# A two-layer hybrid encoder: where the down halves stand among mixed products, new block sizes, and a norm whose shift is taken from three tiles

## Chip, cores and metric

One NeuronCore of one Trainium2 chip. The metric is the device time of one execution in microseconds; lower is better. The kernel before takes 1253.96 us (median of three runs, 1253.59 to 1255.86).

## What is computed

A trunk of two layers on 544 token columns (512 of a prompt, 32 of a later chunk). A layer mixes (gated positions, latent attention and a linear recurrence), projects and normalises, and then runs a convolutional feed-forward part, which the change touches, with a second norm:

```python
up = x @ lp['ffn_w_up']
upc, ffn_conv_new = causal_dwconv(up, ffn_conv_prev, lp['ffn_conv_w'], lp['ffn_conv_b'])
g_ff, val = upc[..., :D_FF], upc[..., D_FF:]
f = (jax.nn.gelu(g_ff) * val) @ lp['ffn_w_down']
x = layer_norm(ALPHA * x + f, lp['ln2_g'], lp['ln2_b'])
```

`D_MODEL` is 1024 (8 tiles of 128 rows), `D_FF` is 2816 (22 tiles for the gate and 22 for the value), the convolution has width 3. All is float32.

## The kernel before, in words

**Precision and units.** Activations stand transposed: 128 features on the partitions, 544 tokens in two column halves of 272 (`HV`). Each float32 operand is split into a high and a low part (`split`, L78: ScalarE copies the high part, L64, VectorE subtracts for the low one, L67), and a product is three matmuls (`mm3`, lines L89 to L91). So a plain tile of the up projection is 8 x 3 = 24 matmuls per half.

**Feed-forward part** (`ffn`, L1086). The 22 gate-and-value pairs are worked in four blocks (`BLK`, L26: 6, 4, 5 and 7 pairs). Block 0 is plain: 12 up tiles, the first five of them on weights that were loaded during the first norm; the others by `unit` (L1189), which also runs `settle`: it finishes the residual tiles of the first norm, and after every second one makes a set of *mixed columns* from two of them (`mixed_x`, L1070: four sums of 272 columns and two splits of 544, tiles ta, tb, th, tl). Pairs of the other blocks are *mixed* (`seven`, L1147): with weights combined by `forms` (L1047: two 512 KB loads, three splits of 128 x 1024, one of 128 x 512 and four sums of 128 x 512 in place, tiles wupr, wfwh, wfwl) a pair takes seven half products of 12 matmuls each, in the order A12, A11, S2, S1, S3, S4, A22. S1, S2, S3 and A22 need the mixed columns. `seven` is a generator and stops twice: after A11 (the second product) and after S3 (the fifth). `post` (L1127) then does the convolution with two scalar_tensor_tensor of VectorE (L70) per tile, the gelu and the product of gate and value, whose split gives the tiles fh and fl.

**Down projection.** A block's down projection (`proj`, L966: eight units of one weight column tile each, two halves per unit, 3 matmuls per pair of the block and half; the weights are split when the unit begins, tiles wd0h to wd7l) runs as `late` during the next block: the loop at L1200 puts some halves at each of the two stops. Of the 16 halves, pair j of nk takes n, by

```python
n = 16 * (j + 1) // nk - 16 * j // nk
for c in ((n + 1) // 2, n // 2):
```

**Second norm** (`proj_ln`, L973, with `LN`, L842). The last block's down projection goes straight into the norm. Tiles 0 and 1 are made together, then 2, then 3, both halves each; `gather` (L868) sums them. After the first half of tile 4 `shift` (L880) makes the mean of the first four tiles by a matmul with ones (lnc) and subtracts it from all eight tiles on VectorE, with squares on ScalarE added up in lnq. Layer 0 does both halves of tile 4, then the first halves of tiles 5 to 7, loads and splits the weights of layer 1's first units (win0 to win2) and does the second halves; in layer 1 tiles 4 to 7 are done so. `stats` (L915) and `apply` (L943) then scale each half; layer 1 stores it. The first norm uses the same class with four tiles.

**Order and buffers.** The kernel is written against a framework that puts the instructions of each engine into an order at compile time, by its own estimate of when operands are ready; program order is the priority, and `tc.high_priority` lifts a few. Buffers are drawn from pools (`BUFS`, L52): five each for split weights (wh, wl), four for raw ones (wr), pages pg, pt, kb and pp. `FPT` (L27) names the pool of each pair's fh and fl. Five PSUM banks serve the products.

Of the kernel before, what the change touches and what calls it, by code (L numbers as in the profile page):

```python
# [9 lines left out]
AF = mybir.ActivationFunctionType  # L10
ALU = mybir.AluOpType
# [8 lines left out]
HW = 272  # L20
# [2 lines left out]
PG = 550  # L23
D_FF = 2816
NI = 22
BLK = ((0, 6), (6, 4), (10, 5), (15, 7))  # L26
FPT = ("", "ggpp", "", "ggppp")  # L27
KO = (0, 2, 4, 6, 1, 3, 5, 7)
ALPHA = (2.0 * DEPTH) ** 0.25
SCALE = 96 ** -0.5  # L30
# [3 lines left out]
C_LN1G, C_LN1B, C_LN2G, C_LN2B = 0, 8, 16, 24  # L34
# [12 lines left out]
def trunk_kernel(ctx: ExitStack, tc: tile.TileContext, i, o, k):  # L47
# [6 lines left out]
    def page(name, dt=F32, tag="pg"):  # L54
        return pool.tile([128, W if tag == "pp" else PG], dt, tag=tag, name=name, bufs=BUFS[tag])

    def bank(name, tag="ps"):
        return psum.tile([128, 512], F32, tag=tag, name=name, bufs={"ps": 5, "ss": 3}[tag])
# [4 lines left out]
    def act(out, in_, func=AF.Copy, **kw):  # L63
        return nc.scalar.activation(out=out, in_=in_, func=func, **kw)  # L64

    def tt(out, a, b, op, e=None):
        return (e or nc.vector).tensor_tensor(out=out, in0=a, in1=b, op=op)  # L67

    def stt(out, a, s, b, op0, op1):
        return nc.vector.scalar_tensor_tensor(out=out, in0=a, scalar=s, in1=b, op0=op0, op1=op1)  # L70
# [67 lines left out]
    xd = [i["x"]] + [dram.tile([8, 128, W], F32, tag=f"xd{l}", name=f"xd{l}") for l in range(1, DEPTH)]  # L138
# [75 lines left out]
    def col_weights(src, kk, name, kper=8):  # L214
        res = []
        for c in range(0, kk, kper):
            n = min(kper, kk - c)
            wh, wl = weights(src[:, 128 * c:128 * (c + n)].rearrange("p (k c) -> p k c", k=n), n, 128, name)
            for j in range(n):
                res.append((wh, wl, j))  # L220
        return res
# [618 lines left out]


    class LN:  # L842
        def __init__(self, xT, first_op, va, cg, cb, spill, final, ns, tag):
            self.x, self.op, self.va, self.cg, self.cb = xT, first_op, va, cg, cb
            self.spill = spill
            self.final = final
            self.n1 = 8 - ns
            self.tag = tag

        def warm(self):  # L850
            t = const([128, 1], F32, "warm")
            act(t, self.c[:, 0:1], AF.Abs_reciprocal_sqrt, scale=0.0, bias=ones[:, 0:1])
# [15 lines left out]
        def gather(self, m, c):  # L868
            if m == 0:
                return  # L870
            if m == 1:
                self.s = page("lns", tag=self.tag)[:, 0:W]
                tt(self.s, self.x[0][:, 0:W], self.x[1][:, 0:W], ALU.add)
                return
            s = self.s[:, c]
            tt(s, s, self.x[m][:, c], ALU.add)
            if m >= 4:
                self.square(m, c)

        def shift(self):  # L880
            s = self.s
            c = self.c = page("lnc", tag=self.tag)[:, 0:W]
            q = self.q = page("lnq", tag=self.tag)[:, 0:W]
            for h in HV:
                b = bank("lnm", "ss")
                nc.tensor.matmul(b[:, 0:HW], ones, s[:, h], start=True, stop=True)
                act(c[:, h], b[:, 0:HW], AF.Copy, scale=1.0 / 512)
            for m in (4, 0, 1, 2, 3, 5, 6, 7):
                x = self.x[m][:, 0:W]
                tt(x, x, c, ALU.subtract)  # L890
                if m == 0:
                    act(q, x, AF.Square)
                elif m in (1, 2, 3):
                    self.square(m, slice(0, W))
            stt(s, c, -4.0, s, ALU.mult, ALU.add)

        def square(self, m, c):
            t = page("lnt", tag="kb")[:, c]
# [74 lines left out]
    def proj_ln(wsrc, kts, ln, name, kper, pre, mid, ko=None):  # L973
        n1 = ln.n1
        ns = 8 - n1

        def get(m):
            w = col_weights(wsrc(m), len(kts), f"{name}{m}", kper)
            return [w[j] for j in ko] if ko else w

        for ms in ((0, 1), (2,), (3,)):
            ws = [get(m) for m in ms]
            for hv in range(2):
                for m, ps in zip(ms, mms(ws, kts, hv)):
                    ln.evac(m, hv, ps)
            if ms[0] == 0 and mid is not None:
                mid()
        def one(m, w, hv):
            ps = mms([w], kts, hv)[0]
            if m == 4 and hv == 0:  # L990
                ln.shift()
            ln.evac(m, hv, ps)

        for m in range(4, n1):
            w = get(m)
            for hv in range(2):
                one(m, w, hv)
        ws = [get(m) for m in range(n1, 8)]
        nxt = pre() if pre is not None else None
        for j in range(ns):  # L1000
            one(n1 + j, ws[j], 0)
            if j == 0:
                ln.warm()
        for j in range(ns):
            ps = mms([ws[j]], kts, 1, (lambda: ln.stats(0)) if j == 0 else ln.head if ln.final and j == ns - 1 else None, 5)[0]
            if j == 0 and not ln.final:
                ln.apply(0, range(4))
            ln.evac(n1 + j, 1, ps)
        if ln.final:
            ln.stats(1)  # L1010
            ln.apply(0)
        else:
            ln.apply(0, range(4, 8))

        def hook():
            if not ln.final:
                ln.stats(1)
            ln.apply(1)
        rest = [] if ln.final else [lambda m=m: ln.settle(m) for m in range(8)]
        return nxt, hook, rest  # L1020

    def wo_stage(l, va, pre):
        xT = []
        for m in range(8):
            x = page(f"xT{m}")
            nc.sync.dma_start(out=x[:, 0:W], in_=xd[l][m])
            if m >= 4:
                act(x[:, 0:W], x[:, 0:W], scale=ALPHA)
            xT.append(x)
        ln = LN(xT, "alpha", va, C_LN1G, C_LN1B, None, False, 3, "pp")  # L1030
        ko = [6, 7, 2, 3, 0, 4, 1, 5]

        kts = [KX[m] for m in ko]
        return xT, *proj_ln(lambda m: i["wo"][l, m], kts, ln, "wo", 8, pre, None, ko)

    def up_w(l, i_, s):
        return col_weights(i["wup"][l, NI * s + i_], 8, "wup", 8)
# [48 lines left out]
    def ffn(l, va, vf, xT, first, hook, rest, pre):  # L1086
# [7 lines left out]
        def settle():  # L1094
            if rest:
                rest.pop(0)()
                if len(rest) % 2 == 0:
                    TX.append(mixed_x(xT, len(TX)))

        late = iter(())  # L1100
        for bl, (i0, nk) in enumerate(BLK):
            fts = {}
# [24 lines left out]
            def post(tl):  # L1127
# [10 lines left out]
                else:  # L1138
                    g = ac.pop((i_, 0))
                    tt(a[:, 0:W], a[:, 0:W], g[:, 0:W], ALU.mult)  # L1140
                    tag = "p" + (FPT[bl] + "tttttt")[i_ - i0]
                    fh, fl = page("fh", F32R, tag), page("fl", F32R, tag)
# [46 lines left out]
            def unit(tl):  # L1189
                n = len(tiles) - tiles.index(tl)  # L1190
                for _ in range(-(-len(rest) // n)):
                    settle()
                w = up_w(l, *tl)
                for hv in range(2):
                    ev(tl, hv, mms([w], KU, hv)[0])

            if bl == 0:
                for tl in tiles[done:]:
                    unit(tl)
            for j in range(nk if bl else 0):  # L1200
                mix = seven(i0 + j)
                n = 16 * (j + 1) // nk - 16 * j // nk
                for c in ((n + 1) // 2, n // 2):
                    next(mix)
                    for _ in range(c):
                        next(late)
                next(mix, None)
# [3 lines left out]

            if bl < len(BLK) - 1:
                def ev2(m, hv, ps, bl=bl):
                    x = xT[m][:, HV[hv]]
                    if bl == 0:
                        stt(x, x, ALPHA, ps, ALU.mult, ALU.add)
                    else:
                        tt(x, x, ps, ALU.add)
                late = proj(wsrc, [fts[j] for j in sorted(fts)], ev2, "wd")
            else:  # L1220
                fin = l == DEPTH - 1

                def mid():
                    nc.sync.dma_start(out=o[7][l], in_=fo)

                ln = LN(xT, "add", va, C_LN2G, C_LN2B, o[0] if fin else xd[l + 1], fin, 4 if fin else 3, "pg")
                nxt = proj_ln(wsrc, [fts[j] for j in sorted(fts)], ln, "wd", 8, pre, mid)
        return nxt

# [10 lines left out]
    for l in range(DEPTH):  # L1240
        mixer(l, nxt, hook, rest)
        va, vf, kvg, sp4 = vecs[l]
        xT, nxt, hook, rest = wo_stage(l, va, lambda: pre_up(l))
# [120 lines left out]
```

## Time and profile before

| | |
|---|---|
| three runs | 1253.59, 1253.96, 1255.86 us |
| the profiled execution | 1253.95 us |
| its span, first to last instruction | 1252.1 us |
| TensorE busy | 1223.2 us (98%), 9305 matmuls |
| VectorE busy | 1013.6 us (81%) |
| ScalarE busy | 741.4 us (59%) |
| mean granted TensorE clock | 0.995 |

All instructions have times from the start of the span. PE is TensorE, DVE VectorE, ACT ScalarE, SP the queue that issues the DMAs. Matmuls are pipelined, so a single one's duration says little; how many fit into a stretch says what one costs. In layer 0 the plain block runs from 239.7 to 307.3 us, block 1 to 386, block 2 to 465.2, block 3 to 572.2, the second norm's stage from there to 632.5. Layer 1 repeats it 617 us later, and its second norm ends the program.

### The profile page before, as it was taken

The numbers are of one execution on the slowest core, as the hardware profiler recorded it, in microseconds if no ns is written. First come the engines' busy times: TensorE is split into PE (matmuls) and PEld (weight loads), VectorE is DVE, ScalarE is ACT, GpSimd is POOL, SyncE is SP. The second block draws the span as 40 slices with busy tenths as digits, with TensorE's granted clock in tenths as the row PEclk, the third lists the DMA queues.
The fourth block names the chain that finished last, engine by engine and source line by source line (L and its number), as shares of the span: only waits on it lengthen the run. The fifth ranks groups of instructions, "written<-read, shape, count | busy, mean of one in ns | idle before, by whom it ended". The sixth has DMA issues, their size and how long they took to land.

```text
span 1252.1 us, 24029 instructions
## 1 busy us (share of the span) xinstructions
PE 1223.2 (98%) x9305; PEld 1178.7 (94%) x9305; DVE 1013.6 (81%) x1932; ACT 741.4 (59%) x1616; POOL 45.7 (4%) x222
## 2 busy tenths in 40 slices
PE   9999999999999999999899999999999999999994
PEld 9999879999999999999899997899999999999994
DVE  6766977997788889886886767689968788898858
ACT  6485874496455655553465767646955455565633
POOL 2400000000000000000000100000000000000000
PEclk9999999999999999999999999999999999999998
DMA  8243434022232332325144423340213223323312
GB/s 284 75 141 98 125 104 161 18 86 72 73 110 83 95 98 89 100 77 170 46 147 136 118 85 113 118 136 18 94 60 105 65 93 93 106 83 106 114 36 73
DMA packets 51043, 125.16 MB, mean 100 GB/s; under 512 B 7784, under 2 KB 13928, under 8 KB 50928
## 3 DMA queue, kind: packets, MB, share of 16 engines
q1 hardware_dynamic: 50928, 123.62, 31.8%
q8 instruction: 73, 1.20, 0.4%
q14 instruction: 42, 0.34, 0.1%
HBM read 113.17 MB, written 5.97 MB: 95 GB/s over the span
## 4 chain that ended last, share of the span: by engine, by line
PE 82%; DVE 8%; ACT 7%; issue 1%; DMA 0%; SPq 0%; ACTq 0%; DVEq 0%
PE mm L89 22%; PE mm L90 21%; PE mm L91 21%; ACT wfwh L64 2%; PE ov L255 2%; DVE xT L70 2%; ACT ac L64 1%; PE ol L255 1%; PE pT L132 1%; ACT xp L64 1%; DVE ac L70 1%; PE s L89 1%; DVE wupr L67 1%; DVE xT L67 1%; PE kv L396 1%
## 5 line engine op out<-in xcount | busy, mean ns | idle before, releaser
L64 ACT ACTIVATE wfwh<-wupr 128x1024 fp32r<-128x1024 f32 (+1 forms) x128 | 121.7, 951 | 122.6 <-PE mm L90 66.1
L67 DVE TENSOR_TENSOR wfwl<-wupr,wfwh 128x1024 fp32r<-128x1024 f32 (+1 forms) x128 | 139.4, 1089 | 14.3 <-ACT wfwh L64 13.0
L89 PE MATMUL mm<-th,wfwh 128*128 128x272 f32 x512 | 148.4, 291 | 0.0
L90 PE MATMUL mm<-tl,wfwh 128*128 128x272 f32 x512 | 147.4, 288 | 0.0
L91 PE MATMUL mm<-th,wfwl 128*128 128x272 f32 x512 | 146.4, 288 | 0.0
L70 DVE SCALAR_TENSOR_TENSOR ac<-xp,vf,ac 128x544 f32<-128x544 f32 x176 | 136.1, 781 | 8.0 <-ACT xp L64 7.2
L90 PE MATMUL mm<-xl,wfwh 128*128 128x272 f32 x384 | 111.1, 289 | 0.0
L91 PE MATMUL mm<-xh,wfwl 128*128 128x272 f32 x384 | 111.1, 289 | 0.0
L89 PE MATMUL mm<-xh,wuph 128*128 128x272 f32 x384 | 109.5, 291 | 1.5 <-DVE xT L67 1.5
L89 PE MATMUL mm<-xh,wfwh 128*128 128x272 f32 x384 | 110.9, 289 | 0.0
L90 PE MATMUL mm<-xl,wuph 128*128 128x272 f32 x384 | 110.3, 289 | 0.0
L91 PE MATMUL mm<-xh,wupl 128*128 128x272 f32 x384 | 110.3, 288 | 0.0
L89 PEld LDWEIGHTS mm<-th,wfwh 128*128 128x128 f32 x512 | 96.3, 188 | 1.2 <-ACT u L64 0.8
L90 PEld LDWEIGHTS mm<-tl,wfwh 128*128 128x128 f32 x512 | 96.6, 189 | 0.0
L91 PEld LDWEIGHTS mm<-th,wfwl 128*128 128x128 f32 x512 | 96.3, 189 | 0.0
L67 DVE TENSOR_TENSOR wupr<-wupr 128x512 f32<-128x512 f32 x128 | 88.2, 689 | 2.4
L89 PEld LDWEIGHTS mm<-xh,wuph 128*128 128x128 f32 x384 | 71.7, 188 | 2.3 <-DVE xT L67 1.9
L91 PEld LDWEIGHTS mm<-xh,wfwl 128*128 128x128 f32 x384 | 72.4, 189 | 0.0
L90 PEld LDWEIGHTS mm<-xl,wuph 128*128 128x128 f32 x384 | 72.4, 189 | 0.0
L89 PEld LDWEIGHTS mm<-xh,wfwh 128*128 128x128 f32 x384 | 72.4, 188 | 0.0
L90 PEld LDWEIGHTS mm<-xl,wfwh 128*128 128x128 f32 x384 | 72.3, 188 | 0.0
L91 PEld LDWEIGHTS mm<-xh,wupl 128*128 128x128 f32 x384 | 72.3, 188 | 0.0
(517 smaller groups left out, 4006.9 us busy)
## 6 DMA issues: line engine op xcount, KB each, us to landing
wupr<-in_wup_dram SPq DMA_DIRECT2D x88, 512.0 KB
xT<-in_x_dram SPq DMA_DIRECT2D x14, 272.0 KB
xd<-xT SPq DMA_DIRECT2D x8, 272.0 KB
xT<-xd SPq DMA_DIRECT2D x8, 272.0 KB
out_dram<-xT SPq DMA_DIRECT2D x16, 136.0 KB
ckT<-in_ckT_dram SPq DMA_DIRECT2D x8, 256.0 KB
cr<-in_ck_dram SPq DMA_DIRECT2D x8, 256.0 KB
win0r<-in_win_dram SPq DMA_DIRECT2D x8, 192.0 KB
```

The lines of the kernel that those rows point to most:

```text
L64: return nc.scalar.activation(out=out, in_=in_, func=func, **kw)
L67: return (e or nc.vector).tensor_tensor(out=out, in0=a, in1=b, op=op)
L70: return nc.vector.scalar_tensor_tensor(out=out, in0=a, scalar=s, in1=b, op0=op0, op1=op1)
L89: nc.tensor.matmul(ps, lh, rh, start=start, stop=False, **kw)
L90: nc.tensor.matmul(ps, lh, rl, start=False, stop=False, **kw)
L91: lastmm[0] = nc.tensor.matmul(ps, ll, rh, start=False, stop=stop, **kw)
L132: nc.tensor.transpose(out, in_, ident[0:p, 0:p])
L255: nc.tensor.matmul(ps, a, b, start=start, stop=stop)
L396: nc.tensor.matmul(b[0:n, 0:288], XL[j][:, cs], wh[:, ci, :], start=False, stop=False)
```

## The change

Blocks are 5, 5, 5 and 7 pairs: one pair per layer passes from the plain block to a mixed one, and `FPT` names a pool for block 1's fifth pair. Of the halves of the previous block's down projection, one stands behind A11 in every pair; the others stand behind S3. The number of halves done by the end of a pair is odd, except after a block's last pair, so that the half behind A11 is the second one of its unit in all pairs but the first of a block. The counts are 3, 4, 2, 4, 3 for five pairs and 3, 2, 2, 2, 2, 2, 3 for seven. The second norm's mean is taken of three tiles, after the first half of tile 3; tile 3 is then gathered and squared like tiles 4 to 7. The first norm stays at four.

```diff
-BLK = ((0, 6), (6, 4), (10, 5), (15, 7))
-FPT = ("", "ggpp", "", "ggppp")
+BLK = ((0, 5), (5, 5), (10, 5), (15, 7))
+FPT = ("", "ggppt", "", "ggppp")
...
             tt(s, s, self.x[m][:, c], ALU.add)
-            if m >= 4:
+            if m >= self.n0:
                 self.square(m, c)
...
         def shift(self):
-            s = self.s
+            s, n0 = self.s, self.n0
...
-                act(c[:, h], b[:, 0:HW], AF.Copy, scale=1.0 / 512)
-            for m in (4, 0, 1, 2, 3, 5, 6, 7):
+                act(c[:, h], b[:, 0:HW], AF.Copy, scale=1.0 / (128 * n0))
+            for m in (n0, *range(n0), *range(n0 + 1, 8)):
...
-                elif m in (1, 2, 3):
+                elif m < n0:
                     self.square(m, slice(0, W))
-            stt(s, c, -4.0, s, ALU.mult, ALU.add)
+            stt(s, c, -float(n0), s, ALU.mult, ALU.add)
...
-        for ms in ((0, 1), (2,), (3,)):
+        n0 = ln.n0
+        for ms in ((0, 1), (2,), (3,))[0:n0 - 1]:
...
-            if m == 4 and hv == 0:
+            if m == n0 and hv == 0:
                 ln.shift()
...
-        for m in range(4, n1):
+        for m in range(n0, n1):
...
+            halves = 0
             for j in range(nk if bl else 0):
                 mix = seven(i0 + j)
-                n = 16 * (j + 1) // nk - 16 * j // nk
-                for c in ((n + 1) // 2, n // 2):
+                end = 16 if j == nk - 1 else 2 * round(8 * (j + 1) / nk - 0.5) + 1
+                for c in (1, end - halves - 1):
                     next(mix)
+                    halves += c
                     for _ in range(c):
                         next(late)
                 next(mix, None)
```

## Rows read from the trace of the kernel before

**Rows 1.** The page's chain of work that ended last, by engine.
```profile
PE 82%; DVE 8%; ACT 7%; issue 1%; DMA 0%; SPq 0%; ACTq 0%; DVEq 0%
```

**Rows 2.** Stretches: us, then busy us (instructions) per engine, clock, DMA share, GB/s.
```profile
core 0: us, PE busy (x) PEld busy (x) DVE busy (x) ACT busy (x) POOL busy (x), PEclk, DMA share, GB/s
239.70:307.30 67.60, 67.60 (x539) 67.54 (x538) 60.37 (x103) 53.82 (x129) 0.90 (x9) 1.00 0.21 67
307.30:386.00 78.70, 78.59 (x626) 78.35 (x625) 60.41 (x90) 39.40 (x77) 0.69 (x7) 1.00 0.26 78
386.00:465.20 79.20, 78.02 (x614) 77.18 (x613) 70.39 (x109) 46.78 (x98) 0.99 (x10) 1.00 0.32 98
465.20:572.20 107.00, 105.98 (x831) 104.51 (x830) 94.28 (x141) 64.06 (x135) 1.94 (x17) 1.00 0.34 102
...
596.40:632.50 36.10, 32.18 (x232) 31.19 (x232) 32.96 (x73) 16.64 (x34) 0.00 (x0) 0.95 0.18 49
...
1213.50:1252.10 38.60, 22.79 (x167) 21.62 (x165) 30.39 (x74) 16.27 (x36) 0.00 (x0) 0.87 0.17 59
```

**Rows 3.** PE's waits: for whom, us in total, times, longest us.
```profile
PE mm L89 <- ACT xh L64: 3.9, 1, 3.9
PE ln L908 <- DVE lns L67: 1.9, 1, 1.9
...
PE mm L89 <- ACT wd3h L64: 1.8, 4, 0.6
```

**Rows 4.** DVE's groups in block 3 of layer 0: busy us, mean ns of one, idle before.
```profile
L67 DVE TENSOR_TENSOR wfwl<-wupr,wfwh 128x1024 fp32r<-128x1024 f32 x19 | 23.2, 1219 | 0.7 <-ACT wfwh L64 0.6
...
L67 DVE TENSOR_TENSOR wupr<-wupr 128x512 f32<-128x512 f32 x24 | 16.5, 688 | 0.4
...
L67 DVE TENSOR_TENSOR xp<-xp,mm 128x272 f32<-128x272 f32 x14 | 6.1, 434 | 6.2 <-PE mm L91 6.2
...
L67 DVE TENSOR_TENSOR wfwl<-wupr,wfwh 128x512 fp32r<-128x512 f32 x6 | 4.2, 693 | 0.2
```

**Rows 5.** DVE's groups in the plain block of layer 0.
```profile
L70 DVE SCALAR_TENSOR_TENSOR ac<-xp,vf,ac 128x544 f32<-128x544 f32 x22 | 16.7, 781 | 0.5 <-ACT xp L64 0.5
L67 DVE TENSOR_TENSOR wupl<-wupr,wuph 128x1024 fp32r<-128x1024 f32 x7 | 8.5, 1220 | 0.0
...
L67 DVE TENSOR_TENSOR tl<-ta,th 128x544 fp32r<-128x544 f32 x4 | 2.9, 720 | 0.0
```

**Rows 6.** Instructions in order of time, block 3, around unit 1 of the down projection.
```profile
482.58 0.73 ACT L64 ACTIVATE wd1h<-wd1r 128x640 fp32r<-128x640 f32 x1
...
483.36 0.39 PE L89 MATMUL mm<-fh,wd1h 128*128 128x272 f32 x1 [0.32 <-ACT wd1h L64]
...
483.71 0.29 PE L89 MATMUL mm<-th,wfwh 128*128 128x272 f32 x1
```

**Rows 7.** Three stretches from A12 to the next pair's A12, block 3, columns as above.
```profile
479.85:494.73 14.88, 14.56 (x117) 14.33 (x115) 13.43 (x21) 8.90 (x20) 0.20 (x2) 1.00 0.30 94
...
526.58:541.14 14.56, 14.56 (x116) 14.38 (x115) 12.57 (x19) 8.56 (x19) 0.20 (x2) 1.00 0.29 96
541.14:555.50 14.36, 14.36 (x116) 14.36 (x115) 12.42 (x20) 8.88 (x21) 0.20 (x2) 1.00 0.32 92
```

**Rows 8.** DVE in order of time, around the plain block's end at 307.3.
```profile
302.45 1.23 DVE L67 TENSOR_TENSOR wfwl<-wupr,wfwh 128x1024 fp32r<-128x1024 f32 x1 [0.82 <-ACT wfwh L64]
...
313.29 0.72 DVE L67 TENSOR_TENSOR fl<-ac,fh 128x544 fp32r<-128x544 f32 x1
```

**Rows 9.** DVE in order of time, second norm of layer 0.
```profile
599.34 3.27 DVE L67 TENSOR_TENSOR xT<-xT,lnc 128x544 f32<-128x544 f32 x5 [3.08 <-ACT lnc L64]
...
614.15 0.43 DVE L67 TENSOR_TENSOR lnq<-lnq,lnt 128x272 f32<-128x272 f32 x1
```

**Rows 10.** The stretch behind PE's wait of 3.9 us, columns as in rows 2.
```profile
620.80:624.40 3.60, 3.60 (x16) 3.36 (x17) 3.60 (x11) 2.48 (x5) 0.00 (x0) 0.55 0.00 0
```

**Rows 11.** DVE in order of time, last norm.
```profile
1216.75 3.27 DVE L67 TENSOR_TENSOR xT<-xT,lnc 128x544 f32<-128x544 f32 x5 [4.21 <-ACT lnc L64]
...
1242.52 4.62 DVE L70 SCALAR_TENSOR_TENSOR xT<-xT,va,lnc 128x272 f32<-128x272 f32 x11
```

More of the change, by code (lines that the diff above doesn't have):

```diff
@@ L842, in trunk_kernel, with __init__ @@
     class LN:
-        def __init__(self, xT, first_op, va, cg, cb, spill, final, ns, tag):
+        def __init__(self, xT, first_op, va, cg, cb, spill, final, ns, tag, n0):
             self.x, self.op, self.va, self.cg, self.cb = xT, first_op, va, cg, cb
@@ L848, in __init__ @@
             self.tag = tag
+            self.n0 = n0
         def warm(self):
@@ L1029, in wo_stage @@
             xT.append(x)
-        ln = LN(xT, "alpha", va, C_LN1G, C_LN1B, None, False, 3, "pp")
+        ln = LN(xT, "alpha", va, C_LN1G, C_LN1B, None, False, 3, "pp", 4)
         ko = [6, 7, 2, 3, 0, 4, 1, 5]
@@ L1224, in mid @@
                     nc.sync.dma_start(out=o[7][l], in_=fo)
-                ln = LN(xT, "add", va, C_LN2G, C_LN2B, o[0] if fin else xd[l + 1], fin, 4 if fin else 3, "pg")
+                ln = LN(xT, "add", va, C_LN2G, C_LN2B, o[0] if fin else xd[l + 1], fin, 4 if fin else 3, "pg", 3)
                 nxt = proj_ln(wsrc, [fts[j] for j in sorted(fts)], ln, "wd", 8, pre, mid)
```

## The prediction

> **What bounds it now.** I read the chain of waits first: 82% of what ended last is TensorE, 8% VectorE, 7% ScalarE [rows 1]. So a change pays if it removes matmuls, or waits of TensorE. The table of stretches says where those are [rows 2]. In layer 0's plain block 539 matmuls take 67.60 us, 0.1254 us each; this is the price of a matmul that never waits. At it block 1 wants 626 x 0.1254 = 78.5 of its 78.7 us (0.2 lost), block 2 wants 77.0 of 79.2 (2.2 lost), block 3 wants 104.2 of 107.0 (2.8 lost): 5.2 us a layer. The two second norms lose most: 232 matmuls in 36.1 us, and 167 in 38.6, with VectorE busy for 32.96 and 30.39 of them. The list of TensorE's waits gives the causes [rows 3]: 3.9 us for the first normed tile in front of layer 1's input projection, 1.9 us for the last norm's sum, and many short ones for down weights not yet split.
>
> **One pair more is mixed.** A plain pair is 4 half tiles of 24 matmuls, 96; a mixed one 7 products of 12, 84. The down products stay at 22 x 8 x 2 x 3 a layer. 2 layers x 12 x 0.1254 = **3.0 us**, all on TensorE's path. VectorE pays by the means of [rows 4, 5]: the mixed pair has three wide splits, one of half width, four sums of 0.69 and three additions of 0.43, 3.66 + 0.69 + 2.75 + 1.30 = 8.4, against 2.44 for the plain pair's two splits: 6.0 more a layer. ScalarE, busy for 64 of 107 us in block 3, hides its part. DMAs: the two 512 KB loads of a pair and the 32 down loads of a layer stay, with widths 5, 5, 5, 7 for 6, 4, 5, 7; POOL's memsets stay at one per tile; on SP's queue the down loads only move among the same neighbours, and TensorE waits for no DMA in its list.
>
> **New down units go behind the fifth product.** Now the counts of halves in block 2 are (2, 1) four times and (2, 2); in block 3 (1, 1), with (2, 1) for the fourth and seventh pair; a new unit often comes first behind A11. The order on TensorE shows the price [rows 6]: the unit's high half is split on ScalarE at 482.58, TensorE waits 0.32 for it, does two of its matmuls and goes over to S2, since the low half is not there. Three pairs of block 3 have 84 + 30 = 114 matmuls, 14.30 us at the price above [rows 7]: with the new unit behind A11 it took 14.88 (0.58 lost), and with the second half behind A11 and the new unit behind S3, which the new rule makes of every pair but each block's first, 14.56 after a pair that split two units and 14.36 otherwise (0.26 and 0.06 lost). New counts are 3, 4, 2, 4, 3 halves in blocks 1 and 2 and 3, 2, 2, 2, 2, 2, 3 in block 3, always one behind A11. Of 17 pairs a layer, 7 follow a pair with two new units (three in blocks 1 and 2 each, one in block 3) and 3 begin a block; I price these ten at 0.26, the other seven at 0.06: 3.0 for 5.2, 2.2 a layer, **4.4 us**. Ends: all at 0.06 gives 4.2 a layer, 8.4; all at 0.58 in block 1, with blocks 2 and 3 as now, costs 2.7 a layer, -5.4. I take the near end because the pairs of rows 7 are the same program in the same block. Behind S3 a late unit would hold S4 and A22, and behind those the next pair's A12; ScalarE's buffer for it comes free after A11, some 6 us earlier.
>
> A block's first half down product still needs the last gated tile. In block 1 its low part ends 314.0 - 307.3 = 6.7 us after the last plain matmul [rows 8], and 24 + 12 matmuls bring TensorE there after 4.5. If nothing stood between, 2.2 us a layer; as in rows 6 the written order can put S2 and S1 there, so 0.26 to 2.2, and I take 0.26 (it is in the sum above).
>
> **The plain block has 10 tiles instead of 12.** VectorE does 60.37 us there in 67.60. Two tiles fewer take away 2 x 1.22 + 4 x 0.78 + 2 x 0.72 = 7.0 [rows 4, 5, 8], leaving 53.4 in 55.6 us: 96%. The four sets of mixed columns (four sums of 0.44 and two splits of 0.72 each, 3.2) fall on five tiles instead of seven. I cost this at nothing. The cover: the last split for the first mixed pair ends at 303.68 [rows 8]; less 7.0 that is 296.7, while S2 needs it 4.9 us (24 + 15 matmuls) after a plain block that ends at 307.3 - 12.0 = 295.3, at 300.2. 3.5 us of cover; each us beyond costs one per layer.
>
> **The second norm's shift comes a tile earlier**, 42 matmuls or 5.27 us. In layer 0 VectorE is idle for 3.08 us before the subtractions at 599.34 and then never until the sums of the first half are ready at 614.58 [rows 9]. With the shift it takes in tile 3's two additions and its sum (0.44 + 0.44 + 0.72) and the split of the first input unit (1.22), 2.8: the sums come 5.27 - 2.8 = 2.4 us sooner, and the wait of 3.9 becomes 1.5. After that wait the granted clock was 0.55, 1.2 GHz for most of 3.6 us, and 16 matmuls were done where 16 x 0.1254 = 2.0 would do [rows 10]: 1.6 lost, of which I count half back, since VectorE feeds these matmuls at about their own rate. Together **3.2 us**; ends 0 and 3.9 + 1.6 = 5.5.
>
> The Trainium skill (TensorE: Matmul & The Clock Gate, Part 1) says that an idle array falls to 1.2 GHz and comes back only with sustained work. Rows 10 agree: 0.55 right after the longest wait. By that rule the whole 1.6 comes back if the shorter wait keeps the clock, and the time would be 0.8 lower, an estimate.
>
> In the last norm the stretch starts at 1216.75 after 4.21 us idle, and the last 11 scalings run from 1242.52 to 1247.14 [rows 11]. The earlier start less tile 3's own work (1.4) is 3.9. From TensorE's side: its wait of 1.9 goes, and three scalings left over from the first half (0.42 each) are done before: 3.1. I take **3.0**; ends 0 (no bank or buffer lets the earlier start through) and 3.9. What is late next is the chain behind the last matmul, which stays.
>
> **Sum.** 3.0 + 4.4 + 3.2 + 3.0 = 13.6. The profiled execution took 1253.95 (span 1252.1 and 1.85 around it), 0.01 under the median: 1253.95 - 13.6 = 1240.4 us.
>
> **Rivals.**
> - *Slower: VectorE holds the first mixed pair.* Place: S2 after the shortened plain block. For it: 96% load, and the same backlog from the first norm in front. Price: were the first pair's weights (3 x 1.22 + 0.69 + 4 x 0.69 = 7.1) and the last mixed columns (4 x 0.44 + 2 x 0.72 = 3.2) done only after the last tile's 6.7 us, S2 would wait 6.7 + 10.3 - 4.9 = 12.1 a layer: 1240.4 + 24.2 = 1264.6. It decides from 8 us a layer (13.6 + 2.5 over two). Against it: 3.5 us of cover. 0.07.
> - *The waits only move.* New units wait behind the fifth product too, and block 1, which has none now, gets 0.58 a pair: 1253.95 - 3.0 + 5.4 - 6.2 = 1250.2. The written order may also override the placing, as in rows 6, so that the change would not do what it says. For: the pair with 14.56. Against: 14.36. 0.14.
> - *The norms gain nothing*, because five PSUM banks fill behind the longer subtractions and TensorE stops instead: 1253.95 - 7.4 = 1246.6. Against: as many half tiles stand between shift and first addition as now. 0.13.
> - My forecast 0.66.
>
> Low end: 3.0 + 8.4 + 5.5 + 3.9 = 20.8, 1233.2; the high end takes in the third rival and most of the second. Range 1234 to 1249. Within 0.2% (2.5 us, about what can be told from no change): 1251.5 to 1256.5. The second rival lies just outside it on the fast side, so part of its chance goes there: faster 0.87, same 0.06, slower 0.07.
>
> **What would show it.** Right: 24 matmuls fewer; no wait for down weights in TensorE's list but at block starts; (1, 1) pairs of 14.4 us; the subtractions about 5 us nearer the block's end; the 3.9 us wait under 2, with a clock near 1.0 after it; no 1.9 us wait at the end. Wrong: a wait of TensorE for the first mixed columns or weights of block 1; waits for down weights behind the fifth product; a wait on VectorE's additions in the norm; pairs of 15 us in block 1.

## The result and the profile after

The changed kernel takes 1240.74 us (median of four runs, 1240.62 to 1241.52) against 1254.1 in the same session: ratio 0.9894, interval 0.9878 to 0.991. The forecast was 1240.4. Its profiled execution took 1240.62, with a span of 1238.5.

From the first matmul of each stage to that of the next, us, both layers:

| stage | before | after | of it matmuls |
|---|---|---|---|
| plain block | 74.26, 74.26 | 62.23, 62.28 | -12.04 each |
| blocks 1 to 3 | 264.88, 265.17 | 273.42, 273.59 | +10.53 each |
| layer 0's second norm, to the first gating unit of layer 1 | 98.21 | 94.17 | 0 |
| last norm, to the end | 62.53 | 60.47 | 0 |

So 3.0 us are matmuls, 4.1 waits of the blocks, 4.0 and 2.1 the two norms: 13.2. (0.5 more in the spans' difference lies ahead of layer 0's plain block, which begins anywhere from 232.2 to 233.1 us in the runs below.)

The page's chain of work that ended last, by engine:

```profile
PE 89%; DVE 6%; ACT 4%; issue 1%; ACTq 0%; DVEq 0%
```

TensorE's share rose from 82% [rows 1]: what is left is more nearly matmuls alone. The stretches that answer to [rows 2], layer 0's plain block, blocks 1, 2, 3 and the norm from the shift on:

```profile
239.20:294.70 55.50, 55.50 (x443) 55.46 (x442) 53.21 (x94) 45.61 (x111) 0.59 (x6) 1.00 0.16 50
294.70:378.70 84.00, 83.69 (x663) 83.10 (x662) 69.12 (x106) 45.79 (x94) 0.99 (x10) 1.00 0.29 89
378.70:462.70 84.00, 83.19 (x663) 82.96 (x662) 73.17 (x111) 49.47 (x100) 0.99 (x10) 1.00 0.30 95
462.70:568.10 105.40, 105.26 (x830) 104.26 (x829) 92.97 (x140) 64.37 (x135) 1.88 (x18) 1.00 0.34 106
...
587.10:628.40 41.30, 39.96 (x307) 38.99 (x306) 38.15 (x84) 19.77 (x40) 0.00 (x0) 1.00 0.22 65
```

The plain block is still without a wait of TensorE, with VectorE busy for 53.21 of 55.50 us (forecast 53.4 of 55.6). At 0.1254 us a matmul the blocks lose 84.00 - 83.1 = 0.9, 0.9 and 105.40 - 104.1 = 1.3: 3.1 us for 5.2, where 3.0 was forecast. TensorE's waits:

```profile
...
PE mm L89 <- DVE xp L67: 1.6, 2, 0.8
PE mm L89 <- DVE xT L67: 1.5, 2, 0.8
PE mm L89 <- ACT xh L64: 1.3, 1, 1.3
PE mm L89 <- ACT fh L64: 0.8, 3, 0.3
```

No wait for split down weights is left [rows 3], nor the 1.9 us for the last sum; the 3.9 us for the first normed tile are 1.3. New are two waits where blocks 1 and 2 begin. In block 2, S2 waits for VectorE's addition into xp, 0.8 in each layer. In block 1, the first down half waits for the last gated tile (fh), 0.3 in each layer. TensorE in order of time: first that down half in block 1, then from A11 to S2 and unit 0 in block 2's first pair:

```profile
300.72 0.39 PE L89 MATMUL mm<-fh,wd0h 128*128 128x272 f32 x1 [0.31 <-ACT fh L64]
...
381.58 0.29 PE L91 MATMUL mm<-xh,wfwl 128*128 128x272 f32 x1
382.68 0.39 PE L89 MATMUL mm<-th,wfwh 128*128 128x272 f32 x1 [0.81 <-DVE xp L67]
382.91 0.29 PE L90 MATMUL mm<-tl,wfwh 128*128 128x272 f32 x1
383.04 0.29 PE L89 MATMUL mm<-fh,wd0h 128*128 128x272 f32 x1
```

Three pairs of block 3, a stretch of 114 matmuls from one pair's S2 to the next pair's, and the stretches around the wait of 1.3 us in layer 0's norm, which answer to [rows 7] and [rows 10]; columns as there:

```profile
479.23:493.55 14.32, 14.32 (x116) 14.32 (x115) 13.43 (x21) 9.26 (x20) 0.20 (x2) 1.00 0.30 98
493.55:507.87 14.32, 14.32 (x116) 14.32 (x115) 13.41 (x21) 9.27 (x20) 0.20 (x2) 1.00 0.29 98
507.87:522.43 14.56, 14.56 (x116) 14.38 (x115) 12.58 (x19) 8.56 (x19) 0.20 (x2) 1.00 0.31 96
...
541.69:556.54 14.85, 14.80 (x117) 14.41 (x115) 12.90 (x21) 8.41 (x19) 0.10 (x1) 1.00 0.31 89
...
611.90:614.00 2.10, 0.81 (x7) 0.59 (x5) 2.10 (x7) 0.57 (x2) 0.00 (x0) 1.00 0.00 0
614.00:617.60 3.60, 3.55 (x26) 3.33 (x27) 3.60 (x10) 2.47 (x5) 0.00 (x0) 1.00 0.00 0
```

The first two pairs take 14.32 us, as good as 114 matmuls (14.30), where [rows 7] had 14.88. Not all of block 3 is like that: the next pair takes 14.56, and the later stretch 14.85, so 0.5 of the block's 1.3 us is lost there. At block 2's start S2 follows A11 with a gap, since unit 0 of the down projection is not split yet (its low part comes at 383.94) and S2 itself waits for VectorE to read A11's bank. Behind the shorter wait of the norm the clock stays at 1.00, and 26 matmuls are done in 3.6 us instead of 16.

### The profile page after: what moved, and what is told of

Same layout as the page of the kernel before. It is cut to its first block, busy times and chain, and to the rows that moved or that the text cites. A ratio compares the mean times of both kernels' runs of the same rounds, so it can differ in the third digit from the quotient of the medians.

```text
span 1238.5 us, 24052 instructions
## 1 busy us (share of the span) xinstructions
PE 1216.6 (98%) x9281; PEld 1173.7 (95%) x9281; DVE 1020.7 (82%) x1950; ACT 745.5 (60%) x1616; POOL 44.8 (4%) x222
## 4 chain that ended last, share of the span: by engine, by line
PE 89%; DVE 6%; ACT 4%; issue 1%; ACTq 0%; DVEq 0%
PE mm L89 24%; PE mm L90 23%; PE mm L91 23%; PE ov L255 2%; DVE xT L70 1%; PE ol L255 1%; PE pT L132 1%; PE s L89 1%; DVE ac L70 1%; PE kv L396 1%; PE s L90 1%; PE kv L395 1%; PE kv L397 1%; PE s L91 1%; ACT wfwh L64 1%
## 5 line engine op out<-in xcount | busy, mean ns | idle before, releaser
L89 PE MATMUL mm<-th,wfwh 128*128 128x272 f32 x544 | 157.8, 290 | 1.6 <-DVE xp L67 1.6
L67 DVE TENSOR_TENSOR wfwl<-wupr,wfwh 128x1024 fp32r<-128x1024 f32 (+1 forms) x136 | 148.1, 1089 | 10.7 <-ACT wfwh L64 7.4
L90 PE MATMUL mm<-tl,wfwh 128*128 128x272 f32 x544 | 156.8, 289 | 0.0
L91 PE MATMUL mm<-th,wfwl 128*128 128x272 f32 x544 | 156.8, 288 | 0.0
L89 PE MATMUL mm<-xh,wuph 128*128 128x272 f32 x320 | 91.0, 291 | 1.5 <-DVE xT L67 1.5
L90 PE MATMUL mm<-xl,wuph 128*128 128x272 f32 x320 | 91.8, 288 | 0.0
L91 PE MATMUL mm<-xh,wupl 128*128 128x272 f32 x320 | 91.7, 288 | 0.0
L64 ACT ACTIVATE xp<-mm 128x272 f32<-128x272 f32 x142 | 55.0, 387 | 24.2 <-PE mm L91 24.0
L67 DVE TENSOR_TENSOR xT<-xT,mm 128x272 f32<-128x272 f32 x112 | 47.2, 434 | 17.7 <-PE mm L91 17.7
L89 PEld LDWEIGHTS mm<-xh,wuph 128*128 128x128 f32 x320 | 59.6, 188 | 2.3 <-DVE xT L67 1.9
```

The lines of the kernel that those rows point to most:

```text
L89: nc.tensor.matmul(ps, lh, rh, start=start, stop=False, **kw)
L90: nc.tensor.matmul(ps, lh, rl, start=False, stop=False, **kw)
L91: lastmm[0] = nc.tensor.matmul(ps, ll, rh, start=False, stop=stop, **kw)
```

## The experiments

All ratios are to the kernel before, timed on the same chip in the same session. The kernel before has medians of 1254.1 to 1255.4 in the sessions, so differences between runs of different sessions are given by the ratios, or by the stages of the profiles.

**One part alone: the norm.** Blocks and placing of before. Against the kernel before, written with the parameter `n0` of the change:

```diff
-                ln = LN(..., fin, 4 if fin else 3, "pg", 4)
+                ln = LN(..., fin, 4 if fin else 3, "pg", 3)
```

> The kernel before, with the second norm's shift taken from three tiles and nothing else. If the norm's gain is its own (theory): 6.2 us less than before, about 1247.9, with TensorE's 3.9 us wait for the first normed tile down to 1.3 to 1.5 and the 1.9 us wait for the last norm's sum gone. Rival, the norm gains only because the block ahead of it hands over sooner: within 1 us of before.

Measured: 1247.99, ratio 0.9945 (0.9933 to 0.9958), 6.9 us less. In its profile the norm's stages take 94.15 and 60.37, as in the changed kernel, and the other stages are those of before within 0.4. The norm's gain is its own.

**One part alone: the placing.** Blocks 6, 4, 5, 7, norm from four tiles, the new rule for the halves.

```diff
-                n = 16 * (j + 1) // nk - 16 * j // nk
-                for c in ((n + 1) // 2, n // 2):
+                end = 16 if j == nk - 1 else 2 * round(8 * (j + 1) / nk - 0.5) + 1
+                for c in (1, end - halves - 1):
```

> The kernel before, blocks 6, 4, 5, 7, with the new placing of the down halves alone. Theory (a new unit behind A11 costs about 0.5 us in the short pairs of blocks 2 and 3): 4 us less, about 1250; block 2 loses under 1 us instead of 2.2, block 3 about 1.2 instead of 2.8. Rival (the waits only move behind the fifth product): within 1 us of before.

Measured: 1248.4, ratio 0.9945 (0.9932 to 0.9957), 6.9 less, 3 more than expected. Blocks 2 and 3 of layer 0:

```profile
386.30:463.60 77.30, 77.30 (x614) 77.06 (x613) 69.69 (x109) 46.19 (x98) 0.99 (x10) 1.00 0.32 98
463.60:569.00 105.40, 105.35 (x831) 104.42 (x830) 93.76 (x141) 64.72 (x136) 1.94 (x18) 1.00 0.34 106
```

Block 2 loses 0.3 (77.30 - 77.0), block 3 1.2. The three blocks take 3.3 us less per layer, 6.6 in all. No wait for split down weights is left in TensorE's list, so the waits do not move behind the fifth product.

**One part alone: the blocks.** 5, 5, 5, 7 and the pools of the changed kernel, with the old placing and the old norm.

```diff
-BLK = ((0, 6), (6, 4), (10, 5), (15, 7))
-FPT = ("", "ggpp", "", "ggppp")
+BLK = ((0, 5), (5, 5), (10, 5), (15, 7))
+FPT = ("", "ggppt", "", "ggppp")
```

> Blocks 5, 5, 5, 7 with the old placing and the old norm. By matmuls alone 3.0 us less, 1251. If short pairs with a new unit behind A11 wait (theory), block 1's pairs, now shorter by 4.5 us, lose up to 0.58 each: 2 us a layer back, so 1253 to 1255. Rival, block 1 has room enough: 1251.

Measured: 1255.05, ratio 1.0005 (0.9996 to 1.0014): nothing. Stretches for blocks 1 and 2:

```profile
294.50:378.50 84.00, 82.82 (x652) 81.81 (x651) 68.93 (x105) 45.93 (x95) 1.00 (x10) 1.00 0.29 89
378.50:465.00 86.50, 85.66 (x673) 84.50 (x673) 73.85 (x112) 49.30 (x100) 0.99 (x10) 1.00 0.31 94
```

The plain block gives back its 12.04 us, and the blocks take 12.3 more a layer where the matmuls make 10.5: 1.8 us of waits a layer eat what the products save. They lie in block 1, which loses 84.00 - 81.8 = 2.2 where it lost 0.2; block 2 loses 2.1 as before. This is what the theory said.

**Two parts: the changed kernel without its norm part.**

```diff
-                ln = LN(..., fin, 4 if fin else 3, "pg", 3)
+                ln = LN(..., fin, 4 if fin else 3, "pg", 4)
```

> The changed kernel without its norm part (shift from four tiles). If the parts add up: 1240.7 + 6.2, about 1247. If the norm's gain depends on the blocks: under 1244 or over 1249.

Measured: 1246.89, ratio 0.9939 (0.9926 to 0.9953), 7.7 less than before. The norm adds up with it: by the ratios 5.6 us lie between this and the changed kernel. But beside the placing alone (6.9) the extra pair and the new blocks bring only about 0.8 of their 3.0 us. The intervals of the two overlap; the plain and mixed stages of the profiles give 0.9.

**Is it the split weights, or one half instead of two?** Odd numbers of halves become even, so that the one half behind A11 always begins a unit.

```diff
-                end = 16 if j == nk - 1 else 2 * round(8 * (j + 1) / nk - 0.5) + 1
+                end = 16 if j == nk - 1 else 2 * round(8 * (j + 1) / nk)
```

> The changed kernel with even numbers of halves by the end of each pair: still one half behind A11, but always the first half of a new unit, whose weights are split just then. Theory (what matters is that the half behind A11 has split weights): the waits of the old placing come back, 0.5 us for each of 14 pairs a layer, 8 to 14 us more, 1249 to 1255. Rival (one half instead of two behind A11 is what matters): within 2 us of 1240.7.

Measured: 1253.24, ratio 0.9985 (0.9976 to 0.9994), 11.4 us above the changed kernel by the ratios (blocks 1 to 3 take 12.2 more in the profiles). TensorE's waits:

```profile
PE mm L89 <- ACT wd6h L64: 5.2, 6, 1.2
PE mm L89 <- ACT wd7h L64: 2.4, 2, 1.2
PE mm L89 <- ACT wd3h L64: 2.1, 6, 0.5
```

It is the split: with the same single half behind A11, the waits for it are back, larger than in [rows 3].

**The new wait: S1 ahead of S2.** S2 adds to A11's bank and S1 opens a bank of its own; the down half moves behind S2.

```diff
-                yield
-                product(b1, f["S2"], t[2])
-                ...
                 b5 = bank("mm")
                 product(b5, f["S1"], t[0], start=True)
+                product(b1, f["S2"], t[2])
+                ...
+                yield
                 product(b1, f["S3"], t[1])
```

> The changed kernel with the products of a pair in the order A12, A11, S1, S2, then one down half, then S3 and the other halves. In the changed kernel 0.6 to 1.0 us is lost at the first S2 of blocks 1 and 2, which adds to the bank of A11 and waits for VectorE to read it; S1 has a bank of its own and would stand in between. Theory (that wait, not the weights, is what the block starts lose): 1 us less per block start in blocks 1 and 2 and a little in block 3, about 4 us in all, 1236.5 to 1238.5. Rival (VectorE is behind there anyway, the wait moves to the next product): within 1 us of 1240.7.

Measured: 1238.0, ratio 0.9861 (0.9846 to 0.9876), 4.1 us better than the changed kernel by the ratios (2.7 by the times, 3.4 by the stages of blocks 1 to 3). The waits for xp are gone from TensorE's list:

```profile
...
PE mm L89 <- DVE xT L67: 1.5, 2, 0.8
PE mm L89 <- ACT xh L64: 1.3, 1, 1.3
PE ln L909 <- DVE lns L67: 0.6, 1, 0.6
...
PE mm L89 <- ACT fh L64: 0.2, 1, 0.2
```

Blocks 1 to 3 take 271.71 us instead of 273.42. The Trainium skill (Perfetto Trace Analysis, Optimizing Tensor Performance) asks for independent products to change PSUM banks, so that reading one overlaps the next; this run agrees, with 1.7 us a layer. Not all of that need be the bank: the edit moves the down half behind S1 and S2 as well, and in block 1 the wait was for fh in front of that half. That wait is gone too (fh has 0.2 for 0.8). No run parts the two; in block 2 the line of the changed kernel names xp, the bank's reader.

**What the extra pair is worth then.** The kernel with S1 ahead of S2, with the blocks of before:

```diff
-BLK = ((0, 5), (5, 5), (10, 5), (15, 7))
-FPT = ("", "ggppt", "", "ggppp")
+BLK = ((0, 6), (6, 4), (10, 5), (15, 7))
+FPT = ("", "ggpp", "", "ggppp")
```

> S1 ahead of S2, the new placing and the norm from three tiles, with the blocks of before, 6, 4, 5, 7. If the extra mixed pair is worth its matmuls once block 1's start no longer waits (theory): 3.0 us more than with 5, 5, 5, 7, about 1241. Rival (the extra pair's worth stays below 1 us, as without S1 first): 1238 to 1239.

Measured: 1240.1, ratio 0.9884 (0.9869 to 0.9898). The pair brings 0.23%, 2.9 us by the ratios (their intervals touch; the profiles' plain and mixed stages differ by 3.0). Without S1 ahead, blocks 1 to 3 of layer 0 take 11.73 us more with the extra pair than without it (273.35 with the norm from four tiles, 261.62 with the placing alone); with S1 ahead 10.56 (271.71 for 261.15), and the matmuls make 10.53. So the waits that S1 ahead of S2 removes, at the starts of blocks 1 and 2, had taken the pair's worth.

**One pair more.** Blocks 4, 6, 5, 7 on the changed kernel.

```diff
-BLK = ((0, 5), (5, 5), (10, 5), (15, 7))
-FPT = ("", "ggppt", "", "ggppp")
+BLK = ((0, 4), (4, 6), (10, 5), (15, 7))
+FPT = ("", "ggpptt", "", "ggppp")
```

> The changed kernel with blocks 4, 6, 5, 7: one pair more passes from the plain block. By matmuls 3.0 us less, 1237.7. Theory of the slower rival of the prediction: VectorE has 46.4 us of work for 43.6 us of plain block, so TensorE waits at the first mixed pair: 1240 to 1246, with a wait of 2 us or more in front of the first S2 of block 1.

Measured: 1249.96, ratio 0.9954 (0.9938 to 0.9971), 7.5 above the changed kernel by the ratios, beyond the range I gave.

```profile
PE mm L91 <- DVE wupl L67: 4.5, 2, 2.3
PE mm L89 <- ACT wfwh L64: 3.8, 2, 1.9
PE mm L89 <- ACT wd0h L64: 1.9, 4, 0.7
```

The first wait is not where I put it: it is inside the plain block, for the low part of a plain tile's own weights (2.3 us per layer). The plain block takes 54.26 us for 50.2 us of matmuls: the wait, and a clock that falls after it. The wait for combined weights (wfwh, 1.9 per layer) stands in block 1's last pair, not at its first. ScalarE and VectorE around the wait in the plain block, the wait in block 1, and the stretches ahead of the first wait and behind it:

```profile
268.29 1.05 ACT L64 ACTIVATE wuph<-wupr 128x1024 fp32r<-128x1024 f32 x1
...
270.80 0.71 DVE L67 TENSOR_TENSOR tl<-tb,th 128x544 fp32r<-128x544 f32 x1
...
272.77 1.22 DVE L67 TENSOR_TENSOR wupl<-wupr,wuph 128x1024 fp32r<-128x1024 f32 x1
...
367.35 0.39 PE L89 MATMUL mm<-th,wfwh 128*128 128x272 f32 x1 [1.92 <-ACT wfwh L64]
```

```profile
257.90:274.00 16.10, 13.88 (x111) 13.66 (x109) 15.84 (x28) 16.07 (x46) 0.40 (x4) 1.00 0.10 35
274.00:278.00 4.00, 3.96 (x20) 3.96 (x21) 4.00 (x8) 3.18 (x7) 0.00 (x0) 0.59 0.27 71
```

The high part is there at 269.34; VectorE then does five other instructions, one of them a split of mixed columns, before it comes to the low part. VectorE is busy for 15.84 of the 16.10 us up to there, and ScalarE, which has to make the high part first, for 16.07: both are full, and which of them would have to be relieved was not tried. In the 4 us behind the first wait 20 matmuls are done, 2.5 us worth at the usual price: 1.5 us of the clock on top of the 2.3. So the load that the slower rival of the prediction feared is real one pair further on, but not its place: the first S2 of block 1 has no such wait.

**Shift from two tiles.**

```diff
-                ln = LN(..., fin, 4 if fin else 3, "pg", 3)
+                ln = LN(..., fin, 4 if fin else 3, "pg", 2)
```

> The changed kernel with the second norm's shift taken from two tiles. Theory (layer 0's norm is bound by VectorE's start, layer 1's last norm since the change by TensorE and the chain behind its last matmul): the 1.3 us wait for the first normed tile goes, 1 to 2 us less in layer 0, under 0.4 in layer 1: 1238.5 to 1240. Rival (PSUM banks fill behind the subtractions): slower by 1 us or more.

Measured: 1239.73, ratio 0.9875 (0.9861 to 0.989). Against the changed kernel's 0.9894 the times do not tell it apart; the stages do: layer 0's norm 92.79 for 94.17, with no wait for the first normed tile in the list, the last norm 60.39 for 60.47. Both as expected: the first was still waiting for VectorE, the second no longer.

**Together.** S1 ahead of S2, as above, and the shift from two tiles; against the kernel with S1 ahead:

```diff
-                ln = LN(..., fin, 4 if fin else 3, "pg", 3)
+                ln = LN(..., fin, 4 if fin else 3, "pg", 2)
```

> S1 ahead of S2 and the shift from two tiles together, on the changed kernel. If the two gains lie in different stages and add up: 1238.0 - 1.0, about 1237. Rival (the earlier hand-over of block 3 already feeds the norm): 1238.

Measured: 1236.52, ratio 0.9853 (0.9836 to 0.9869). Better than the kernel before and the changed one; against S1 first alone (0.9861) the times leave it open, while the stage of the norm again takes 92.80 for 94.15.

## Why the prediction was right, step by step

- *One pair more, 3.0 us.* Right for the matmuls: 9281 for 9305, and the plain block shrank by 12.03 and 11.98 us for 12.04. The cover held: VectorE needed 53.21 us and TensorE never waited in it. What I did not see is that the pair's worth would be eaten elsewhere.
- *The blocks' waits, 4.4 us.* Measured 4.1, and per block 0.9, 0.9, 1.3 where I had 1.1, 1.1, 0.8. The sum is right, the reasons only half. I priced a pair after one with two new units at 0.26; most such pairs lose nothing, and the pair of block 3 that takes 14.56 follows one that began a single unit, so what I read into [rows 7] as the cause was not it. The placing alone gains 6.6 in the blocks, more than I gave it. Against that stands what I priced too low: a block's start. In block 2 S2 waits there for VectorE's reading of A11's bank: two down halves stood in between, now it is one, and that one is not ready. In block 1 I named the late gated tile (0.26 to 2.2) and took the low end; it stands in the list of waits with 0.3 a time (fh). That the bank itself would be waited for, 0.8 us in block 2, I did not name; TensorE's list shows it, and the run with S1 first is without it. That the sum came out at 4.1 for 4.4 is luck: pairs priced too high and starts priced too low nearly cancel.
- *Layer 0's norm, 3.2 us.* Measured 4.0. The step was right in size: 2.4 us sooner by my sum, and the wait went from 3.9 to 1.3. I counted half of the clock's 1.6 us back. The clock stayed at 1.00 and nearly all of it came back, as the rule that I had set beside it (the Trainium skill, TensorE: Matmul & The Clock Gate, Part 1) says.
- *Last norm, 3.0 us.* Measured 2.1. The wait of 1.9 went; of the three scalings left over only one did. I took it that VectorE would do them before the last tile came. They stand behind the sums of the last tiles in VectorE's order, and two are still left when the second half's subtractions end:

```profile
1223.14 2.15 DVE L70 SCALAR_TENSOR_TENSOR xT<-xT,va,lnc 128x272 f32<-128x272 f32 x5
...
1229.39 4.21 DVE L70 SCALAR_TENSOR_TENSOR xT<-xT,va,lnc 128x272 f32<-128x272 f32 x10
```

  The scalings at the end are 10 for 11 [rows 11]. TensorE is the bound up to its last matmul: no wait of it is left there, and an earlier shift, from two tiles, brings nothing more (60.39 for 60.47).
- *The rivals.* The waits did not move (placing alone), the norms gained (norm alone), VectorE did not hold the first mixed pair, though with one pair fewer in the plain block the low part of a plain tile comes late. The total came closer than its terms, by luck: 0.9 too much in the last norm stands against 0.8 too little in the first.

## What to carry to other kernels

When a stage is interleaved with another one's products, put behind a short gap only work whose operands are split already, and let new operands begin where their engines are idle; here that alone was half of the gain, and without it, in the run of the blocks alone, an arithmetic saving of 3 us was worth nothing. After every such move look at what used to hide behind the work that left: here S2 came 1.1 us after A11's last matmul on the same bank (381.58 and 382.68), and another product put between them removed the wait. And before a faster form takes more of a stage, sum up the other engines' work in what is left: 96% of VectorE's time went well, one pair more, with ScalarE as full as VectorE, did not.

## What was not expected of the hardware

The same wait of 1.9 us before the last sums did two things to TensorE's clock. In the kernel before, the eight short matmuls behind it ran at the upper level. In the profiled run of the blocks alone they took about twice as long, 0.45 us each for 0.23, with a granted clock of 0.53 in that stretch, most of it at 1.2 GHz (first TensorE in order of time, then the stretch):

```profile
1237.42 1.22 PE L908 MATMUL ln<-lns,ones 128*128 128x272 f32 x2 [1.90 <-DVE lns L67]
1238.43 1.11 PE L908 MATMUL ln<-lnq,ones 128*128 128x272 f32 x2
1239.34 1.11 PE L921 MATMUL ln<-xT,ones 128*128 128x272 f32 x2
1240.25 0.93 PE L922 MATMUL ln<-lnt,ones 128*128 128x272 f32 x2
```

```profile
1237.40:1241.00 3.60, 3.58 (x8) 2.49 (x8) 2.30 (x7) 1.42 (x5) 0.00 (x0) 0.53 0.22 77
```

Its last norm took 63.94 us for 62.53, and the one of the placing alone 63.96 with the same wait. So such a wait costs 1.9 or 3.3 us, and the change takes both away. The length of the wait alone does not decide it: after 1.90 (the blocks alone) and 1.93 (the placing alone) the clock fell, after 1.94 (before) and 1.92 (one pair more, 367.35) it stayed at 1.00. After the waits of 1.3 us it stayed at 1.00, and after those of 2.3 (one pair more) and 3.9 [rows 10] it was 0.59 and 0.55. The wait of 3.9 us does not cost the same everywhere either: with 3.92 in each run, layer 0's norm stage took 98.21 us before and 99.19 with the blocks alone, where the clock was still at 0.67 in the second 3.6 us, for 0.98 before (first the row of before, then that of the blocks alone):

```profile
624.40:628.00 3.60, 3.60 (x27) 3.45 (x27) 3.60 (x11) 2.77 (x7) 0.00 (x0) 0.98 0.02 5
...
624.10:627.70 3.60, 3.60 (x19) 3.44 (x19) 3.20 (x9) 1.77 (x5) 0.00 (x0) 0.67 0.02 5
```

What decides was not tried.
